# Keeping one FFN operand set on chip, and giving all attention score rows the two-bank PSUM buffers

## The chip, the cores and the metric

One core of a Trainium2 chip runs the whole kernel. The metric is the device time in microseconds (us). TensorE (PE in the rows, PEld its weight loads), VectorE (DVE), ScalarE (ACT), GpSimd (POOL) and SyncE (SP, which issues every DMA) each work through a list of instructions that was fixed when the kernel was built; they meet through semaphores.

## What is computed

One decoder layer for 1,024 positions of width 1,024, in float32. Cut to what matters here:

```
u = rmsnorm(x);  z = u @ w_in                      # input projections
y_rnn = rglru(z...);  y_att = causal_attention(...)  # 8 heads, blocks of 128 queries
h = x + concat(rmsnorm(y_rnn), rmsnorm(y_att)) @ w_out
v = rmsnorm(h)
h = h + (silu(v @ w_gate) * (v @ w_up)) @ w_down   # D_FF = 2816 = 22 blocks of 128
h = h + sigmoid(rmsnorm(h) @ w_ple_gate) * rmsnorm(p @ w_ple_proj)
out = rmsnorm(h)
```

## The kernel before, in words

**Order of the work.** Everything is recorded first as a list of operations (`Plan.add`, L203) and then ordered by `Plan.order` (L239), a list scheduler. It simulates the five engines with a cost per operation (`Plan.cost`, L167) and a latency from engine to engine (`LAT`, L133). Whenever an engine is free it takes the ready operation with the lowest place in the program whose buffers are free, and the order that comes out is what the engines get. A cost in the plan changes no instruction, only the order. `Plan.order` also hands out the buffers, of two kinds that matter here. SBUF has 51 "slots" of 128 x 1024 float32. PSUM is cut into four single banks of 512 columns (tag `bank`) and two double banks of 1024 columns (tag `wide`, `NWIDE = 2`). Every instruction is issued at L361, so the rows are told apart by the names of tiles.

**Attention** (L840 to L1050). For each of the 8 heads and each of the 8 query blocks `qb`, `scores` (L877) writes a score row of (qb+1) x 128 columns to a PSUM tile `s`: the query and the key are each split into a high and a low float32r part, so three products per 512 columns, and one 128-column bf16 product that adds the causal mask. VectorE then takes the row's maximum (`nm`), and ScalarE the exponential into `pA` (blocks 0 to 3) or `pB` (blocks 4 to 7). Rows of up to 512 columns (blocks 0 to 3) are put into a single bank, the longer ones into a double bank (L888). The single banks also hold the transposed probabilities (`tp`, copied out to `pt`), the product with the values (`av`, added into `ya`), and the query, key and value projections (`qps`, `kps`, `v`).

**The output projection.** `o_rnn` (L978) fetches the weights of output block n with `weight(("wo", n), 1)`: this block and the one behind it in the list of weights. Behind the last block of `wo` stands the first of `wpp`, which is used only after the FFN; its high and low halves stay in two slots from there on.

**The FFN** takes 22 blocks of 128 in 11 pairs p. Each 2 x 2 block product is done with seven products in place of eight (`products`, L1145): operand combinations are prepared on VectorE and ScalarE, and the seven results are added into place. For each pair, `ff_gate` and `ff_up` run seven products each; the result is two slots, from which `make_x` (L1088) prepares seven operands for the down projection, each a high and a low half in one slot named `hx` (`hilo`: an ACT copy and a DVE subtraction; four further DVE combinations, named `vt` and `silu`). `spill(p)` writes an operand to a DRAM tile, also named `hx`, one per step of the next pair's up products; for the last pair (10), whose operands have no following pair, the loop `while spill(NF // 2 - 1)` (L1283) writes all seven behind the last up product.

**The down projection** runs over chunks of pairs, `CHUNKS = ((0,1), (2,3), (4,5,6), (7,8,9,10))`. In each chunk, m = 0 to 3 runs seven products per pair of output blocks (`down`, L1238), and each product is added into the residual rows `h` on VectorE. The rows `h` come back from DRAM (`h<-hd`), two for each m of chunk 0. The operands of a chunk are fetched from DRAM (`fetch`, L1233) while the chunk before runs; those of chunk 0 during the last two up pairs (`mid_x`, L1265). The down weights `wd` are loaded and split as the products need them (`pump`). Down products also write to PSUM tiles `ff_z`, `ff_y` and `ff_x`; `ff_z` takes four of the seven products, added up in PSUM, and is read into `h` after each, so the second product into `ff_z` waits until VectorE has added the first to `h`.

All DMAs go through SP in the planned order: one that waits for its data or its slot holds up all that are behind it.

Of the kernel before, what the change touches and what calls it, by code (L numbers as in the profile page):

```python
# [19 lines left out]
HB = 512  # L20
NH = 8
DFF = 2816
NF = DFF // P
# [12 lines left out]
LAG = 3  # L36
FFW = False
CH = [slice(a, b) for a, b in [(0, 512), (512, 768), (768, 1024)]]
CHUNKS = ((0, 1), (2, 3), (4, 5, 6), (7, 8, 9, 10))
KEEP = ()  # L40
MX = (2, 4, 6)
GL = (3, 5)
NO = [0, 4, 1, 5, 2, 6, 3, 7]
# [97 lines left out]
class Plan:  # L141
# [25 lines left out]
    def cost(self, eng, fn, a, k, out):  # L167
        w = out.width() if isinstance(out, View) else 0
        if fn == "dma_start":
            v = k["out"] if isinstance(k["out"], View) else k["in_"]  # L170
            return v.shape[0] * v.width() * 4 / 360e3, 2.1
        if eng == "tensor":
            if fn == "transpose":
                return 0.108, 0.18
            return w * 0.000417 + 0.0135, 0.18
        if eng == "vector":
            if fn == "reciprocal":
                return 0.065 + w * 0.0063, 0.13
            if fn in ("tensor_reduce", "reduce_sum"):
                return 0.065 + k["in_"].width() * 0.00104, 0.13  # L180
            ptr = 0.061 * any(isinstance(x, View) for x in (k.get("scalar"), *a[2:])) if fn == "scalar_tensor_tensor" else 0.0
            one = fn in ("tensor_copy", "tensor_scalar", "tensor_scalar_mul", "tensor_scalar_add", "tensor_scalar_max")
            if one and all(v.buf.tag not in PS for v in [*a, *k.values()] if isinstance(v, View)):
                return 0.068 + w * 0.00052, 0.13
            return 0.068 + ptr + w * 0.00104, 0.13
        if eng == "scalar":
            src = k["in_"] if "in_" in k else a[1]
            c = (0.052 if src.buf.tag in PS else 0.093) + w * 0.000833
            c += 0.093 * sum(isinstance(k.get(n), View) for n in ("scale", "bias"))
            c += 0.2 * isinstance(k.get("accum_out"), View)  # L190
            return c, 0.14
        return 0.15 + w * (0.0033 if fn == "tensor_copy" else 0.0022), 0.14
# [10 lines left out]
    def add(self, eng, fn, a, k):  # L203
        o = Op()
        o.eng, o.fn, o.a, o.k, o.idx = eng, fn, a, k, len(self.ops)
        o.succ, o.npred, o.ready = [], 0, 0.0
        out = k["out"] if "out" in k else a[0]
        outs = [v for v in (out, k.get("accum_out")) if isinstance(v, View)]
        rest = list(a[1:] if "out" not in k else a) + [v for n, v in k.items() if n not in ("out", "accum_out")]
        ins = [v for v in rest if isinstance(v, View)]  # L210
        o.cost, o.lat = self.cost(eng, fn, a, k, out)
        o.port = self.shares(eng, fn, ins)
        f = k.get("func") or next((x for x in a if isinstance(x, AF)), None)
        o.table = f.name if eng == "scalar" and f is not None and f.name in FIRST else None
        preds = {self.hold: True} if self.hold else {}
        for v, w in [(v, False) for v in ins] + [(v, True) for v in outs]:
            p0, p1, c0, c1 = v.region
            keep = []
            for (q, r, qw) in v.buf.log:
                hit = r[0] < p1 and p0 < r[1] and r[2] < c1 and c0 < r[3]  # L220
                if hit and (w or qw) and q is not o:
                    preds[q] = True
                if not (w and q is not o and p0 <= r[0] and r[1] <= p1 and c0 <= r[2] and r[3] <= c1):
                    keep.append((q, r, qw))
            keep.append((o, v.region, w))
            v.buf.log = keep
        o.key = o.idx + self.shift + OFF.get(eng[0] + out.buf.name.rstrip('_ab') if isinstance(out, View) else '', 0) + (DEF if eng in ('vector', 'scalar') and not any(v.buf.tag == 'bank' for v in ins + outs) else 0)
        o.bufs = list(dict.fromkeys(v.buf for v in ins + outs))
        for b in o.bufs:
            if not b.left:  # L230
                b.first = o.idx
            b.left += 1
        for q in preds:
            q.succ.append(o)
            o.npred += 1
        self.ops.append(o)
        return o

    def order(self):  # L239
# [28 lines left out]
        while left:  # L268
            while frees and frees[0][0] <= t:
                _, _, tag, n = heapq.heappop(frees)  # L270
                free[tag] += n
            moved = False
            for e in names:
                while future[e] and future[e][0][0] <= t:
                    _, i, o = heapq.heappop(future[e])
# [5 lines left out]
                while avail[e] and tries < 40:  # L281
                    i, _, o = heapq.heappop(avail[e])
# [20 lines left out]
                o = best[2]  # L303
# [22 lines left out]
                left -= 1  # L326
                for b in o.bufs:
                    b.left -= 1
                    b.done = max(getattr(b, "done", 0.0), o.end)
                    if not b.left:  # L330
                        heapq.heappush(frees, (b.done, b.pos, b.tag, 1))
                for s in o.succ:
# [44 lines left out]
def hybrid_layer(ctx, tc, xT, pT, pos, vec, const, const2, w1, wn, wrg, wq, wkv, wo, wg, wu, *rest):  # L377
# [19 lines left out]
    def bank(name):  # L397
        return plan.tile(psp, [P, HB], F32, name, "bank", 8 - 2 * NWIDE)

    def wide(name):  # L400

        return plan.tile(psp, [P, S], F32, name, "wide", NWIDE)
# [474 lines left out]
    def scores(hd, qb):  # L877
        if qb == 0:
            pA, pA3 = slot("pA"), slot("pA3")
            st[hd] = {"p": {0: pA[:, 0:128], 1: pA[:, 128:384], 2: pA[:, 384:768], 3: pA3[:, 0:512]},  # L880
                      "rs": small([P, 8], "rs"), "nm": small([P, 8], "nm")}
        if qb >= 4:
            st[hd]["p"][qb] = slot("pB")
        pd, rs, nm = st[hd]["p"][qb], st[hd]["rs"], st[hd]["nm"]
        (qh, ql), (kh, kl) = qs[hd], ks[hd]
        n = (qb + 1) * P
        cc = slice(qb * P, (qb + 1) * P)
        ps = wide("s") if n > HB else bank("s")  # L888
        for c0 in range(0, n, HB):
            c1 = min(c0 + HB, n)  # L890
            T.matmul(ps[:, c0:c1], lhsT=qh[:, cc], rhs=kh[:, c0:c1], start=True, stop=False)
            T.matmul(ps[:, c0:c1], lhsT=qh[:, cc], rhs=kl[:, c0:c1], start=False, stop=False)
            if c1 == n:
                T.matmul(ps[:, n - P:n], lhsT=ib, rhs=mb, start=False, stop=False)
            T.matmul(ps[:, c0:c1], lhsT=ql[:, cc], rhs=kh[:, c0:c1], start=False, stop=True)
        V.tensor_reduce(out=nm[:, qb:qb + 1], in_=ps[:, :n], axis=AX.X, op=ALU.max, negate=True)
        A.activation(pd[:, :n], ps[:, :n], AF.Exp, bias=nm[:, qb:qb + 1], accum_out=rs[:, qb:qb + 1])
# [79 lines left out]

    def o_rnn(n, pss, k):  # L978
        if n not in wos:
            wos[n] = weight(("wo", n), 1)  # L980
            ops[n] = pss()
        c = slice(k * P, (k + 1) * P)
        mm(ops[n][:2], wos[n][0][:, c], wos[n][1][:, c], ys[k], k == 0, False)
# [43 lines left out]
    n = 0  # L1027
# [162 lines left out]
    def ff_up(p, mid):  # L1190
        s = sil.pop(p)
        u = [slot("ff_u"), slot("ff_u")]

        def ahead(i):
            pump("u", p)
            if i >= 3:
                if p + 1 < NF // 2:
                    pump("g", p + 1)
                else:
                    pump("d", 0)  # L1200
            if p:
                spill(p - 1)
            mid(i)

        def sink(i, ps):
            r, h = PART[i]
            v, x = u[r][:, HS[h]], s[r][:, HS[h]]
            if i < 3:
                A.activation(v, ps, AF.Copy)
            elif i == 6:  # L1210
                V.tensor_mul(x, ps, x)
            else:
                V.tensor_add(v, ps, v)
                V.tensor_mul(x, v, x)

        products(fw["u", p][0], xfs, sink, ahead)
        spilling[p] = make_x(s[0], s[1], "hx"), []
        hx[p] = spilling[p][1]


    spilling, hx = {}, {}

    def spill(p):
        steps, made = spilling[p]
# [40 lines left out]
    def mid_x(c, span):  # L1265

        ps = list(CHUNKS[c]) if c < len(CHUNKS) else []
        nxt.extend([None] * 7 for _ in ps)
        todo = [(i, k) for i in range(7) for k in range(len(ps))]
        n = len(todo)  # L1270

        def mid(m, i):
            at = span - (3 - m) * 7 - 6 + i
            while todo and (n - len(todo)) * span < at * n:
                a, k = todo.pop(0)
                nxt[k][a] = fetch(ps[k], a)
        return mid

    first = mid_x(0, 14)
    for p in range(NF // 2):  # L1280
        ff_gate(p)
        ff_up(p, (lambda i: first(p - NF // 2 + 4, i)) if p >= NF // 2 - 2 else lambda i: None)
    while spill(NF // 2 - 1):  # L1283
        pass


    hg, pacc = [], []
# [212 lines left out]
```

## Time and profile before

| | us |
|---|---|
| median of 3 runs (lowest, highest) | 1231.26 (1230.91, 1231.33) |
| the profiled execution | 1228.91 |
| its span, from the first to the last instruction | 1227.1 |
| TensorE busy in it | 1172.6 |
| VectorE, ScalarE, GpSimd busy | 990.7, 648.5, 249.8 |
| moved by DMA | 165.35 MB |

The profiled execution lies 2.35 us below the median of the runs, and its span 1.81 us below its own time; the rows are microseconds from the start of the span. The matmul rows of one instruction last longer than the distance to the next, because they are pipelined. In the windows, a granted TensorE clock of 1.00 is 2.4 GHz and 0.50 is 1.2 GHz.

### The profile page before, as it was taken

The page shows a single profiled execution, that of the slowest core. Times are in us where ns is not written, and L with a number is a line of the kernel's source. Part 1 is how long each engine was busy: PE and PEld are TensorE (multiplying, and loading weights), DVE is VectorE, ACT ScalarE, POOL GpSimd, SP SyncE. Part 2 cuts the span into 40 slices and gives each one's busy share as a digit, 9 for nine tenths or more (in the row PEclk, how much of TensorE's full clock was granted, in tenths as well). Part 3 has the DMA queues.
Part 4 walks back from the last instruction along what each step waited for, and adds up shares of the span by engine and source line. Part 5 has one row for each costly group of instructions (what it writes and reads, how often), then busy time and mean ns, then how long its engine had stood idle before and what let it go on. Part 6 is the DMA issues. An engine that isn't in the chain of part 4 may idle for free.

```text
span 1227.1 us, 15468 instructions
## 1 busy us (share of the span) xinstructions
PE 1172.6 (96%) x5608; PEld 967.8 (79%) x5608; DVE 990.7 (81%) x1486; ACT 648.5 (53%) x1086; POOL 249.8 (20%) x149
## 2 busy tenths in 40 slices
PE   8999999999999999999999999999599999999995
PEld 6788777878778878888888888888488887887894
DVE  7878777777888699988888888867689758776998
ACT  8347857777855365454454444444232213476665
POOL 0001220322101123333113332133000000243042
PEclk9999999999999999999999999999799999999998
DMA  8001100000214231453434434465998774122362
GB/s 333 18 18 35 35 1 1 1 1 1 87 69 155 103 121 54 170 189 120 172 122 160 182 124 167 155 220 188 382 374 289 276 253 176 35 103 90 117 206 87
DMA packets 50268, 165.35 MB, mean 135 GB/s; under 512 B 5648, under 2 KB 8976, under 8 KB 50192
## 3 DMA queue, kind: packets, MB, share of 16 engines
q1 hardware_dynamic: 50192, 164.37, 36.7%
q8 instruction: 44, 0.72, 0.2%
q14 instruction: 32, 0.26, 0.1%
HBM read 115.58 MB, written 48.76 MB: 134 GB/s over the span
## 4 chain that ended last, share of the span: by engine, by line
PE 76%; DVE 12%; ACT 5%; issue 3%; DMA 3%; POOL 1%; SPq 0%; DVEq 0%; ACTq 0%; POOLq 0%
PE ff_z L361 27%; PE ff_y L361 14%; PE ff_x L361 6%; PE wo L361 4%; PE plg L361 4%; PE wn L361 4%; PE s L361 3%; PE tp L361 2%; PE av L361 2%; DMA wd_r<-in_wd 2%; PE qps L361 2%; PE wn_b L361 1%; DVE h L361 1%; PE wn_a L361 1%; PE wo_a L361 1%
## 5 line engine op out<-in xcount | busy, mean ns | idle before, releaser
L361 POOL TENSOR_TENSOR silu<-silu,nf_rb 128x512 f32<-128x512 f32 x77 | 119.8, 1580 | 280.1 <-DVE silu L361 257.9
L361 PE MATMUL ff_z<-hx,wd 128*128 128x512 f32 x528 | 129.6, 393 | 9.8 <-DVE h L361 8.1
L361 PE MATMUL ff_z<-x,wg 128*128 128x512 f32 x528 | 128.0, 390 | 0.2
L361 PE MATMUL ff_z<-x,wu 128*128 128x512 f32 x528 | 127.0, 389 | 0.9 <-DVE ff_u L361 0.9
L361 PEld LDWEIGHTS ff_z<-hx,wd 128*128 128x128 f32 x528 | 99.7, 189 | 31.9 <-DVE h L361 8.8
L361 PEld LDWEIGHTS ff_z<-x,wu 128*128 128x128 f32 x528 | 99.0, 188 | 21.9 <-DVE ff_u L361 1.3
L361 PEld LDWEIGHTS ff_z<-x,wg 128*128 128x128 f32 x528 | 98.9, 188 | 21.8 <-DVE x L361 1.1
L361 DVE TENSOR_TENSOR h<-ff_z,h 128x512 f32<-128x512 f32 x64 | 44.1, 690 | 33.7 <-PE ff_z L361 25.6
L361 ACT ACTIVATE wd<-wd_r 128x256 fp32r<-128x256 f32 (+2 forms) x64 | 29.8, 490 | 73.6 <-DMA wd_r<-in_wd 26.3
L361 PE MATMUL ff_y<-hx,wd 128*128 128x512 f32 x264 | 66.3, 394 | 0.1
L361 POOL TENSOR_TENSOR p_acc<-p_acc,sq 128x1024 f32<-128x1024 f32 x7 | 18.2, 2596 | 231.8 <-ACT sq L361 231.8
L361 PE MATMUL ff_y<-x,wg 128*128 128x512 f32 x264 | 64.3, 390 | 0.9 <-ACT x L361 0.9
L361 PE MATMUL ff_y<-x,wu 128*128 128x512 f32 x264 | 63.4, 389 | 0.0
L361 PE MATMUL plg<-hg_h,wpg_l 128*128 128x256 f32 (+1 forms) x192 | 61.4, 320 | 1.3 <-DVE wpg_l L361 1.2
L361 PE MATMUL plg<-hg_h,wpg_h 128*128 128x256 f32 (+1 forms) x192 | 61.5, 320 | 0.3 <-ACT np_rb L361 0.3
L361 PE MATMUL plg<-hg_l,wpg_h 128*128 128x256 f32 (+1 forms) x192 | 61.3, 319 | 0.0
L361 PEld LDWEIGHTS ff_y<-hx,wd 128*128 128x128 f32 x264 | 50.2, 191 | 11.4 <-ACT wd L361 0.9
L361 PEld LDWEIGHTS ff_y<-x,wg 128*128 128x128 f32 x264 | 49.4, 188 | 11.7 <-ACT x L361 1.3
L361 ACT ACTIVATE wd<-wd_s 128x256 fp32r<-128x256 f32 (+2 forms) x48 | 23.3, 496 | 66.1 <-DVE wd_s L361 50.6
L361 DVE TENSOR_TENSOR pt<-tp,pt 128x512 fp32r<-128x512 f32 (+1 forms) x96 | 50.3, 549 | 9.6 <-ACT pt L361 9.3
L361 PEld LDWEIGHTS ff_y<-x,wu 128*128 128x128 f32 x264 | 49.6, 188 | 10.3
L361 DVE TENSOR_REDUCE nm<-s 128x1 f32<-128x128 f32 (+3 forms) x64 | 47.8, 752 | 11.7 <-PE s L361 10.8
(407 smaller groups left out, 3041.0 us busy)
## 6 DMA issues: line engine op xcount, KB each, us to landing
hx<-hx SPq DMA_DIRECT2D x154, 512.0 KB, 3.9
wpg_raw<-in_wpg SPq DMA_DIRECT2D x24, 512.0 KB, 3.5
wg_r<-in_wg SPq DMA_DIRECT2D x22, 512.0 KB, 4.6
wu_r<-in_wu SPq DMA_DIRECT2D x22, 512.0 KB, 4.1
wn_raw<-in_wn SPq DMA_DIRECT2D x10, 512.0 KB, 7.2
wo_raw<-in_wo SPq DMA_DIRECT2D x8, 512.0 KB, 4.0
h<-in_xT SPq DMA_DIRECT2D x8, 512.0 KB, 4.2
hd<-h SPq DMA_DIRECT2D x8, 512.0 KB, 2.9
```

Of the source, the lines that this page charges most:

```text
L361: getattr(self.engines[o.eng], o.fn)(*a, **k)
```

## The change

Four things are edited. All score rows take a double bank. In the plan's model, a matmul costs at least 0.113 us, an operation on VectorE or ScalarE whose input and output start on different partitions costs 0.11 us more, and a PSUM buffer comes free by the latency from the reading engine to TensorE. The seven operands of up pair 10 are neither written to DRAM nor fetched: they stay in their slots, and pair 10 joins pair 2 in the second down chunk (the down weights are laid out to fit, on the host). The last block of `wo` no longer asks for the first block of `wpp`, so that this is loaded with the rest of `wpp` after the FFN.

```diff
-CHUNKS = ((0, 1), (2, 3), (4, 5, 6), (7, 8, 9, 10))
-KEEP = ()
+CHUNKS = ((0, 1), (2, 10), (3, 4, 5), (6, 7, 8, 9))
+KEEP = (10,)
...
-            return w * 0.000417 + 0.0135, 0.18
+            return max(w * 0.000417 + 0.0135, 0.113), 0.18
...
+        if eng in ("vector", "scalar") and any(v.region[0] != outs[0].region[0] for v in ins if v.width() > 8):
+            o.cost += 0.11
...
-                    b.done = max(getattr(b, "done", 0.0), o.end)
+                    b.done = max(getattr(b, "done", 0.0), start + c + LAT[e, "tensor"] if b.tag in PS and e != "tensor" else o.end)
...
-        ps = wide("s") if n > HB else bank("s")
+        ps = wide("s")
...
-            wos[n] = weight(("wo", n), 1)
+            wos[n] = weight(("wo", n), 1 if n != NO[-1] else 0)
...
-            if p:
+            if p and p - 1 not in KEEP:
                 spill(p - 1)
...
-        spilling[p] = make_x(s[0], s[1], "hx"), []
+        steps = make_x(s[0], s[1], "hx")
+        if p in KEEP:
+            kept[p] = steps
+            return
+        spilling[p] = steps, []
         hx[p] = spilling[p][1]
...
-    spilling, hx = {}, {}
+    spilling, hx, kept = {}, {}, {}
...
         nxt.extend([None] * 7 for _ in ps)
-        todo = [(i, k) for i in range(7) for k in range(len(ps))]
+        nxt[:] = [kept[p] if p in KEEP else x for p, x in zip(ps, nxt)]
+        todo = [(i, k) for i in range(7) for k in range(len(ps)) if ps[k] not in KEEP]
...
-    while spill(NF // 2 - 1):
-        pass
+    for p in KEEP:
+        kept[p] = list(kept[p])
```

## Rows read from the trace of the kernel before

**Rows 1.** The page: the span, and each engine's busy time.

```profile
span 1227.1 us, 15468 instructions
PE 1172.6 (96%) x5608; PEld 967.8 (79%) x5608; DVE 990.7 (81%) x1486; ACT 648.5 (53%) x1086; POOL 249.8 (20%) x149
```

**Rows 2.** TensorE's waits, whole span: total us, times, longest.

```profile
PE ff_z L361 <- DVE h L361: 8.1, 1, 8.1
PE no_ms L361 <- DVE o_acc L361: 6.8, 1, 6.8
...
PE ff_x L361 <- DVE wd L361: 4.5, 1, 4.5
...
PE ff_z L361 <- ACT wd L361: 1.7, 1, 1.7
```

**Rows 3.** Stretches: length, engines busy (PE, PEld, DVE, ACT, POOL), clock, DMA share, GB/s.

```profile
862.80:870.60 7.80, 3.33 (x15) 2.44 (x13) 7.80 (x16) 3.67 (x6) 0.00 (x0) 1.00 0.91 358
870.60:880.28 9.68, 1.58 (x5) 0.78 (x5) 1.58 (x3) 0.00 (x0) 0.00 (x0) 0.53 0.99 369
880.28:885.30 5.02, 5.02 (x13) 4.01 (x14) 2.98 (x6) 1.47 (x4) 0.00 (x0) 0.54 1.04 423
885.30:961.00 75.70, 75.70 (x334) 62.19 (x332) 66.63 (x143) 22.88 (x57) 0.00 (x0) 1.00 0.93 344
```

**Rows 4.** Timeline, 862 to 886: start, length, instructions; in brackets the idle time before.

```profile
861.75 10.93 SPq L361 DMA_DIRECT2D hx<-hx  x9
...
862.80 1.52 PE L361 MATMUL ff_z<-hx,wd 128*128 128x512 f32 x6
...
870.61 1.58 PE L361 MATMUL ff_x<-hx,wd 128*128 128x512 f32 x4 [4.47 <-DVE wd L361]
870.79 0.70 DVE L361 TENSOR_TENSOR hx<-silu,hx 128x512 fp32r<-128x512 f32 x1
872.77 2.34 SPq L361 DMA_DIRECT2D h<-hd  x2
...
879.53 0.69 DVE L361 TENSOR_TENSOR h<-ff_z,h 128x512 f32<-128x512 f32 x1 [8.04 <-DMA h<-hd]
...
880.28 2.93 PE L361 MATMUL ff_z<-hx,wd 128*128 128x512 f32 x6 [8.09 <-DVE h L361]
```

**Rows 5.** SP's own waits, 841 to 872: total us, times, longest.

```profile
SPq L361 <- DVE hx L361: 27.7, 10, 13.6
```

**Rows 6.** The eight loads of h, 860 to 905: issue to landing.

```profile
DMA to landing us min/median/max: 6.7/7.6/8.8
```

**Rows 7.** Stretches in the attention, columns as in rows 3.

```profile
171.47:174.88 3.41, 3.41 (x11) 2.56 (x10) 0.46 (x3) 2.00 (x5) 2.37 (x1) 0.50 0.02 5
209.01:212.43 3.42, 3.42 (x13) 2.50 (x13) 2.35 (x5) 1.39 (x6) 0.00 (x0) 0.50 0.00 0
165.00:341.00 176.00, 167.59 (x982) 135.93 (x981) 138.25 (x239) 134.32 (x284) 38.52 (x24) 0.98 0.06 19
```

**Rows 8.** TensorE's waits ahead of score rows, 165 to 341.

```profile
PE s L361 <- DVE v L361: 1.8, 1, 1.8
PE s L361 <- ACT pA L361: 1.4, 3, 0.6
...
PE s L361 <- DVE ya L361: 0.8, 1, 0.8
PE s L361 <- DVE pt L361: 0.8, 2, 0.4
```

**Rows 9.** Readers of the score rows: ns min/median/max of one, first and last start.

```profile
L361 DVE TENSOR_REDUCE nm<-s x64: 280/748/1226, 167.7 to 335.5; 128x1 f32<-128x128 f32 x8, 128x1 f32<-128x256 f32 x8, 128x1 f32<-128x384 f32 x8, 128x1 f32<-128x512 f32 x8
L361 ACT ACTIVATE pA<-s,nm x32: 358/526/711, 170.5 to 320.6; 128x128 f32<-128x128 f32 x8, 128x256 f32<-128x256 f32 x8, 128x384 f32<-128x384 f32 x8, 128x512 f32<-128x512 f32 x8
...
L361 ACT ACTIVATE pB<-s,nm x32: 783/970/1133, 183.3 to 337.1; 128x640 f32<-128x640 f32 x8, 128x768 f32<-128x768 f32 x8, 128x896 f32<-128x896 f32 x8, 128x1024 f32<-128x1024 f32 x8
```

**Rows 10.** The split of the two wpp blocks on VectorE: ns min/median/max, first and last start.

```profile
L361 DVE TENSOR_TENSOR wpp_l<-wpp_raw,wpp_h x2: 1210/1218/1225, 407.5 to 1087.9; 128x1024 fp32r<-128x1024 f32 x2
```

## The prediction

> **What bounds the kernel now.** The page comes first: TensorE is busy for 1172.6 of 1227.1 us [rows 1], so all that can be won without removing matmuls is the rest, some 54 us, and what a low clock costs. I then listed what TensorE waits for [rows 2]. Of the larger waits, two (8.1 and 4.5 us) lie where the up products end and the down products begin; a third, 6.8 us for o_acc, is the tail of the kernel, which the change doesn't touch; a fourth, 1.7 us for wd, lies at the start of the fourth down chunk.
>
> The windows around the first down products [rows 3] show the place. From 862.8 to 870.6 VectorE has no free moment while TensorE works for 3.33 of 7.80 us. From 870.6 to 880.28 all compute engines all but stand still beside the DMA engines (share 0.99), and TensorE's clock is at its lower level nearly throughout. From 885.3 on TensorE has no gap for 75.7 us. The timeline says why [rows 4]. The down products start at 862.80 and stop for 4.47 us at a wd half whose subtraction stands on VectorE behind the operands of pair 10. The next product into ff_z must wait until the first has been added to h. The h rows are only asked for at 872.77: on SP their loads stand behind nine hx transfers, from 861.75 on. The load lands 6.7 us after its issue (the shortest of eight) [rows 6], the addition starts at 879.53, and TensorE goes on at 880.28 after 8.09 us [rows 4]. SP itself is held up by VectorE: between 841 and 872 it spends 27.7 us in ten waits for hx operands that it is to write out [rows 5]. The last operand of pair 10 is made at 870.79 to 871.49, and only then can its write go out, with the h loads behind it. So this stall is a queue on SP whose head waits for VectorE.
>
> **Part 1: pair 10 stays on chip.** Seven writes and seven reads of 512 KB leave SP's queue, each with its wait; no instruction on TensorE, VectorE or ScalarE goes. The h loads then stand behind the fourteen fetches of chunk 0 alone. Those need slots that the up products give back as they end, so the last can go out near 863, and the h loads right behind. With the same 6.7 us they land near 870 [rows 6]. What is late next is VectorE: its subtractions for pair 10 keep their place in the program and end at 871.5 [rows 4]. The addition to h takes 0.69 us, so TensorE takes up ff_z at about 872.3 instead of 880.28: 8.0 us. The 4.47 us wait for wd stays, since the work ahead of it on VectorE is unchanged.
>
> The clock: before, it is at 0.53 and 0.54 in the windows where TensorE works for 1.58 and 5.02 us [rows 3], which costs 0.47 x 1.58 + 0.46 x 5.02 = 3.0 us. After a wait of 4.47 us I expect one short drop still. The shortest in these rows is 3.41 us at 0.50 [rows 7], worth 1.7 us, so 1.3 us come back. Sum for this part: 9.3 us.
>
> Bounds: nothing, if the planner issues the h loads no earlier, since it fixes SP's order from its own model; up to 4.5 + 8.1 + 3.0 = 15.6 us if the new order also brings the wd subtraction ahead of pair 10's. I take 9.3, because VectorE's queue of 7.8 us without a gap [rows 3] is untouched. A loss is bounded by slots: seven stay taken from about 871 to the end of the second chunk. But that chunk needs these operands in slots anyway, seven fetches for it fall away, and the two wpp slots come free.
>
> The 1.7 us at the fourth chunk [rows 2] depends on 28 fetches, all still there: 0 to 1.7, taken as 0.
>
> **Part 2: wpp later.** One load, one ScalarE copy and one VectorE subtraction of 1.22 us [rows 10] move from about 400 us to just before the products that use them. On SP the load passes all FFN loads and stands between p and the second wpp block. The second block's subtraction is the row at 1087.9, and TensorE is at down products until about 1090, which covers it. Without that cover the cost is the 1.22 us of VectorE. I take 0; range 0 to 1.2 us lost.
>
> **Part 3: score rows in double banks, and the new costs in the plan.** No instruction changes. TensorE idles 8.4 us of the 176 in the attention [rows 7]. Of that, 4.8 us are score rows of up to 512 columns that wait until a single bank has been read by another engine: v, ya, pt and pA name its earlier holder [rows 8]. The clock is low twice, for 3.41 and 3.42 us [rows 7], which costs 1.7 us each time; in both stretches TensorE worked without a gap. The most that can be won is 8.4 + 3.4 = 11.8 us.
>
> Against it stands the new wait. A short row now needs one of two double banks, and on TensorE's list everything behind it waits with it: the transposes, the value products, the next projections. From the readers' rows, a buffer is held for reduction and exponential: about 0.28 + 0.36 to 0.69 + 0.71 us for short rows and up to 1.23 + 1.13 for long ones [rows 9], and the matmuls ahead of these. I estimate 2 us for a short and 3.7 us for a long row: 32 x 3.7 = 118 us of 2 x 176 us before, 182 us of it after, so 34% becomes 52%. The double banks aren't full, and VectorE and ScalarE, at 138 and 134 of 176 us [rows 7], set the pace of a row. I take 3.5 us won: two single waits gone (1.8 and 0.8 us), one low-clock stretch less (1.7), and 0.8 us of new waits. Ends: 11.8 us won, and the loss of rival 3.
>
> A rule speaks against this part. The Trainium skill ("TensorE: Matmul & The Clock Gate", section "A second HAM failure mode: psum-queue depth-cycling") says that a kernel which cycles through PSUM buffers, with short idle times between groups of matmuls, can see its clock go down and up again and again. Two buffers in turn for 64 rows are such a cycle. The trace has only two drops in eight heads, in spite of seven short waits [rows 8], so it bears that out weakly. By that rule the 1.7 us counted above would go and the 10 us of drops in rival 3 would come.
>
> **Sum.** 9.3 + 0 + 3.5 = 12.8 us. The profiled execution took 1228.91 us, 1.8 more than its span and 2.35 less than the median, so it would become 1216.1, and the median 1231.26 becomes 1218.5.
>
> **Rivals.**
> (1) The attention gains more: with four banks free for transposes and value products, most of its idle time and both drops go, 10 us instead of 3.5. For it: nearly all the larger waits for score rows are for single banks. Against: VectorE and ScalarE are near 80%. Time: 1212.
> (2) The stall only moves: the h loads go out earlier but land behind full DMA queues (share 0.91 to 1.04 [rows 3]), or VectorE adds to h only after further wd halves. Then 3 of the 9.3 us are won; with 3.5 from the attention, 1225.
> (3) Slower: the double banks become the wait. Each of 32 short rows holds TensorE until one comes free. The gain of part 1 is used up at 9.3 / 32 = 0.29 us per row. At 0.4 us per row it is 12.8 us, and with a clock drop in each of the eight heads instead of two in all, another 6 x 1.7 = 10 us: 1231.26 - 9.3 + 23 = 1245. For it: the occupation rises by half. Against: at 52% one of the two is mostly free, and the planner knows when.
> (4) The change doesn't do what it says: pair 10 stays on chip, but SP's planned order keeps the h loads behind slots that are late. About 1231.
>
> **How the numbers follow.** My forecast has 0.55, rival 1 0.17, rival 2 0.13, rival 3 0.09, rival 4 0.06. The first alone spans 1213 to 1224. For 8 in 10 the range takes in rivals 1 and 2, the first with 11.8 us in the attention and 10.8 in part 1 as its far end, the second with nothing in the attention: 1208 to 1229. 0.2% is 2.5 us, about what a measurement of this kernel can tell from no change. Faster by over that: forecast, rival 1, and nearly all of rival 2, 0.84. Within: rival 4 and some of rival 2, 0.07. Slower: rival 3, 0.09.
>
> **What would show it.** In the changed profile, SP's waits for hx between the last up and the first down products should be fewer by seven, with the h loads issued near 863 to 866. The wait of ff_z for h should be under 2 us, with the wait of ff_x for wd still near 4.5, and the low-clock stretch after it short. HBM traffic should fall by 14 x 512 KB. In the attention, waits of s should name exponentials of score rows alone, and their sum should stay under 4 us. It would be wrong if the wait for h stays above 5 us, or if TensorE's idle time between 165 and 341 grows.

## The result, and the profile after

The changed kernel takes 1209.14 us (median of 4 runs, 1206.05 to 1209.53) against 1231.09 us for the kernel before in the same session: a ratio of 0.9819, 95% interval 0.9801 to 0.9838. It is 22.0 us faster. The forecast was 1218.5 us, 12.8 us faster, with a range of 1208 to 1229.

The page of the profiled execution (1206.05 us, the fastest of the four), the lines that answer to [rows 1], and its HBM line:

```profile
span 1204.2 us, 15416 instructions
PE 1164.7 (97%) x5608; PEld 965.5 (80%) x5608; DVE 985.5 (82%) x1486; ACT 645.5 (54%) x1086; POOL 250.8 (21%) x149
HBM read 111.91 MB, written 45.09 MB: 130 GB/s over the span
```

TensorE does the same 5608 matmuls and is busy for 7.9 us less; that is a first hint of where the forecast was short. HBM reads are down from 115.58 to 111.91 MB and writes from 48.76 to 45.09 MB, 3.67 MB each, seven operands of 512 KB.

TensorE's waits over the whole span (total us, times, longest), against [rows 2]:

```profile
PE no_ms L364 <- DVE o_acc L364: 6.7, 1, 6.7
...
PE ff_z L364 <- DVE h L364: 5.2, 2, 4.2
...
PE ff_z L364 <- ACT wd L364: 0.9, 1, 0.9
```

The wait for h has halved, and the wait of ff_x for wd is gone. The timeline at the first down products, against [rows 4]:

```profile
846.80 1.62 SPq L364 DMA_DIRECT2D h<-hd  x2
...
849.30 1.52 PE L364 MATMUL ff_z<-hx,wd 128*128 128x512 f32 x6
...
850.60 0.42 DVE L364 TENSOR_TENSOR wd<-wd_r,wd 128x256 fp32r<-128x256 f32 x1
...
852.02 1.52 PE L364 MATMUL ff_x<-hx,wd 128*128 128x512 f32 x6
...
856.35 0.69 DVE L364 TENSOR_TENSOR silu<-silu,vt 128x512 f32<-128x512 f32 x1
...
856.95 0.69 DVE L364 TENSOR_TENSOR h<-ff_z,h 128x512 f32<-128x512 f32 x1
...
857.70 2.93 PE L364 MATMUL ff_z<-hx,wd 128*128 128x512 f32 x6 [4.15 <-DVE h L364]
```

The h loads go out 2.5 us before the first down product, where before it was 10 us after it. The first wd half that ff_x was late for is now split ahead of pair 10's operands, so ff_x runs at once. The addition to h starts when VectorE has done the operand ahead of it, with no idle time between.

SP's own waits for operands that it is to write out, from 828 to 858, a stretch that lies around the first down product as that of [rows 5] does:

```profile
SPq L364 <- DVE hx L364: 2.3, 3, 1.3
```

Ten such waits (27.7 us) have become three.

The stretches, columns as in [rows 3]: the attention, from the first score product to the end of the last row's maximum, the low-clock stretch at the down products, and all from 10.67 us to the next fall of the clock, with that fall in the last row.

```profile
168.40:323.40 155.00, 153.32 (x942) 127.94 (x941) 131.33 (x232) 125.63 (x273) 36.07 (x22) 1.00 0.05 16
...
857.18:860.59 3.41, 2.89 (x7) 2.32 (x8) 2.33 (x5) 1.92 (x5) 0.00 (x0) 0.50 1.02 414
...
10.67:352.00 341.33, 333.14 (x1779) 275.32 (x1778) 286.50 (x440) 243.41 (x416) 55.05 (x30) 1.00 0.12 46
352.00:355.41 3.41, 2.89 (x7) 2.31 (x8) 3.41 (x4) 2.75 (x3) 0.00 (x0) 0.50 0.00 0
```

For the same stretch of the attention, the kernel before shows:

```profile
167.10:336.80 169.70, 161.29 (x946) 130.58 (x945) 132.49 (x232) 129.14 (x275) 36.81 (x22) 0.98 0.05 16
```

So this stretch is 14.7 us shorter, and the clock no longer falls in it. But it doesn't hold quite the same work: six products of the value projection (`v`) that lie inside it before, behind the first score product, stand ahead of its start after, which is 1.4 us. Stretches with the same work, 1100 matmuls in either kernel (the rows count two more at the edges), go from the first `v` product to the first product that uses the attention's result (`wo<-ya_h`), first before, then after:

```profile
165.13:366.57 201.44, 190.54 (x1102) 154.59 (x1100) 157.97 (x270) 145.95 (x302) 38.39 (x24) 0.98 0.07 24
164.97:352.52 187.55, 183.32 (x1102) 152.46 (x1100) 156.33 (x270) 144.41 (x302) 37.75 (x24) 1.00 0.08 26
```

This is the gain of the attention without work that only moved: 13.9 us, of which 6.7 are idle time (10.9 against 4.2) and 7.2 busy time of the same matmuls. From the first down product to the first product of the per-layer embedding (`ple`), the kernel before took 228.1 us (862.80 to 1090.89) and the changed one 218.4 (849.30 to 1067.68).

### The profile page after: what moved, and what is told of

Read it like the earlier page. It is cut to its first block, busy times and chain, and to the rows that moved or that the text cites. A ratio compares the mean times of both kernels' runs of the same rounds, so it can differ in the third digit from the quotient of the medians.

```text
span 1204.2 us, 15416 instructions
## 1 busy us (share of the span) xinstructions
PE 1164.7 (97%) x5608; PEld 965.5 (80%) x5608; DVE 985.5 (82%) x1486; ACT 645.5 (54%) x1086; POOL 250.8 (21%) x149
## 3 DMA queue, kind: packets, MB, share of 16 engines
HBM read 111.91 MB, written 45.09 MB: 130 GB/s over the span
## 4 chain that ended last, share of the span: by engine, by line
PE 82%; DVE 10%; ACT 3%; issue 2%; DMA 2%; SPq 0%; DVEq 0%; ACTq 0%
PE ff_z L364 28%; PE ff_y L364 14%; PE ff_x L364 7%; PE plg L364 6%; PE wo L364 5%; PE s L364 4%; PE wn L364 4%; PE av L364 2%; PE tp L364 2%; PE qps L364 2%; DMA wd_r<-in_wd 2%; PE wn_b L364 1%; DVE h L364 1%; PE wn_a L364 1%; PE wo_a L364 1%
## 5 line engine op out<-in xcount | busy, mean ns | idle before, releaser
L364 ACT ACTIVATE wu<-wu_r 128x512 fp32r<-128x512 f32 x44 | 27.6, 627 | 59.2 <-DVE wu_r L364 28.1
```

Of the source, the lines that this page charges most:

```text
L364: getattr(self.engines[o.eng], o.fn)(*a, **k)
```

## The experiments

"Before" below is always the kernel before, run on the same chip in the same session; its median was 1229.99 to 1230.29 us in the three sessions. The attention is timed from the first score product to the end of the last row's maximum, the down stage from the first down product to the first ple product.

### The double banks alone

```diff
-        ps = wide("s") if n > HB else bank("s")
+        ps = wide("s")
```

> The kernel before, with all score rows in the double banks and nothing else. Theory A (the single banks were the attention's limit): the output projection's first product with the attention's result starts 10 to 14 us earlier than before (366.6 us), waits of s for readers of v, ya and pt are gone, the total falls by 10 to 14 us. Theory B (the plan's new costs made the gain, the buffers alone are worth little): that start moves by under 4 us, the total by under 4 us or up, since the planner still thinks narrow matmuls shorter than they are. The wait at the first down products stays near 12.6 us in both.

1220.74 us, ratio 0.9915 (0.9882 to 0.9948), about 10 us faster. The attention fell from 169.6 to 156.3 us. Its window, that of the 1100 matmuls, and TensorE's waits in the first:

```profile
170.70:327.10 156.40, 154.22 (x946) 128.42 (x945) 131.29 (x233) 125.88 (x275) 36.01 (x22) 1.00 0.05 15
167.31:356.16 188.85, 183.80 (x1101) 152.52 (x1100) 156.62 (x270) 144.33 (x302) 36.02 (x23) 1.00 0.08 26
```

```profile
PE tp L361 <- DVE k_l L361: 0.8, 2, 0.5
PE v L361 <- DVE v L361: 0.5, 1, 0.5
PE tp L361 <- DVE ya L361: 0.4, 1, 0.4
```

No score row waits any more [rows 8], and no new wait for a double bank has come. The same 1100 matmuls take 188.85 us where they took 201.44: 12.6 us less, 5.9 of it idle time and 6.7 busy time. The first product with the attention's result starts at 356.2 instead of 366.6, 10.4 us earlier: in this profile the attention itself starts 2.2 us later, behind a low-clock stretch (3.41 us from 152.51) that the profile before doesn't have. Theory A stands, with the total at its lower end: this one line makes nearly all of the attention's gain. The waits of 12 us at the down products were still there (4.5 and 7.3 us).

### The plan's new costs alone

```diff
-            return w * 0.000417 + 0.0135, 0.18
+            return max(w * 0.000417 + 0.0135, 0.113), 0.18
...
+        if eng in ("vector", "scalar") and any(v.region[0] != outs[0].region[0] for v in ins if v.width() > 8):
+            o.cost += 0.11
...
-                    b.done = max(getattr(b, "done", 0.0), o.end)
+                    b.done = max(getattr(b, "done", 0.0), start + c + LAT[e, "tensor"] if b.tag in PS and e != "tensor" else o.end)
```

> The kernel before, with the three edits of the plan's model and nothing else. Theory A: the attention ends within 4 us of before, the waits of s for v, ya and pt are still there. Theory B: it ends 10 to 14 us earlier, with those waits mostly gone. The wait at the first down products stays near 12.6 us in both.

1230.12 us, ratio 0.9998 (0.9981 to 1.0014): nothing. The attention took 170.4 us (the 1100 matmuls 201.44, exactly as before), with the waits for single banks grown where the reader is a score row's exponential:

```profile
PE s L364 <- ACT pA L364: 4.0, 5, 1.0
PE s L364 <- ACT q_h L364: 1.6, 1, 1.6
PE s L364 <- DVE v L364: 1.5, 1, 1.5
PE qps L364 <- ACT pA L364: 1.4, 1, 1.4
```

A better model of the durations did not find an order that the buffers don't allow. Theory B falls.

### The kept pair alone

```diff
-CHUNKS = ((0, 1), (2, 3), (4, 5, 6), (7, 8, 9, 10))
-KEEP = ()
+CHUNKS = ((0, 1), (2, 10), (3, 4, 5), (6, 7, 8, 9))
+KEEP = (10,)
...
-    while spill(NF // 2 - 1):
-        pass
+    for p in KEEP:
+        kept[p] = list(kept[p])
```

> The kernel before, with pair 10 kept on chip in the second chunk and nothing else (wpp still loaded early, old costs, short score rows in single banks). Theory A (the h loads stood behind writes on SP that waited for VectorE): the total falls by 8 to 11 us, all of it between the first and the last product of chunk 0, and the attention is as before. Rival (the removal works only with the two slots of wpp or the new order): under 4 us, since the h loads still go out after 868 us.

1222.97 us, ratio 0.9943 (0.9926 to 0.9959): 7.0 us faster. The down stage fell from 228.1 to 222.6 us in the profiled execution, which was the slowest of its runs (1225.84). TensorE's waits from 840 to 1000, and its low-clock stretch:

```profile
PE ff_x L361 <- DVE wd L361: 4.5, 1, 4.5
PE ff_y L361 <- DVE h L361: 0.9, 1, 0.9
```

```profile
870.51:877.34 6.83, 4.49 (x11) 3.52 (x12) 5.00 (x11) 1.70 (x4) 0.00 (x0) 0.50 1.03 413
```

The wait of 8.1 us for h is gone and the one of 4.5 us for wd stays, as the prediction had it; the first h load goes out at 864.86, 0.2 us before the first down product, and lands 6.7 us later. The gain lies under the 8 to 11 us of theory A, though well above the rival's 4. In this profile two things are short of what was forecast. TensorE's idle time in the down stage fell by 6.0 us (from 14.4 to 8.4), not by 8.0. And the clock stays low for 6.83 us, not for one 3.41, and falls again for 3.41 us at 1010.46: TensorE works for 4.49 and 3.41 us of these, which costs 4.0 us against 3.0 before, where 1.3 were to come back.

### Double banks and costs together

```diff
-CHUNKS = ((0, 1), (2, 10), (3, 4, 5), (6, 7, 8, 9))
-KEEP = (10,)
+CHUNKS = ((0, 1), (2, 3), (4, 5, 6), (7, 8, 9, 10))
+KEEP = ()
...
-            wos[n] = weight(("wo", n), 1 if n != NO[-1] else 0)
+            wos[n] = weight(("wo", n), 1)
```

(against the changed kernel)

> The changed kernel without the kept pair and without the later load of wpp: double banks and new costs alone. If the parts add, the total is 11 to 14 us under the kernel before and the waits of the first down products are near 12.6 us again. If score rows and costs work against each other apart and gain only together, this run is faster than both single ones together.

1217.75 us, ratio 0.9897 (0.9873 to 0.9921), 12.4 us faster. The attention took 154.9 us, 1.4 less than with the double banks alone, so the costs are worth that much once the buffers are there (the 1100 matmuls: 187.48 against 188.85). The totals of the two runs differ by 3.0 us; the other 1.6 can't be told from the spread of the double banks' own executions (1215.32 to 1222.68). The waits at the down products were 4.5 and 7.9 us. With the 7.0 us of the kept pair the parts add up to 19.4 of the 22.0 us; the rest is no larger than the intervals of the three ratios, 2 to 3 us to either side.

### The first wpp block, early or late

Two runs: the changed kernel with the early load, and the kernel before with the kept pair and the late load.

```diff
-            wos[n] = weight(("wo", n), 1 if n != NO[-1] else 0)
+            wos[n] = weight(("wo", n), 1)
```

> The changed kernel with the first wpp block loaded early again, so that its two halves hold two slots through the FFN. If the later load is worth nothing by itself (my prediction), the total stays within 2 us of the changed kernel and TensorE has no wait of over 2 us for wd. Rival: the two free slots let SP's fetches and wd loads go earlier, and it was this that removed the 4.5 us wait for wd and shortened the low clock; then that wait is back and the stretch from the first down product to the first ple product grows from 218.4 to near 222.6 us, as in the run with the kept pair alone.

> The kernel before with the kept pair and the later load of wpp, short score rows in single banks and old costs. If the two slots make the difference of 4 us between the kept pair alone (222.6 us from the first down product to the first ple product) and the changed kernel (218.4), it is near 218.4 here, and the wait for wd is gone. If the new costs make it, it stays near 222.6 with the 4.5 us wait for wd.

They took 1209.33 us (0.9824, 0.9789 to 0.9859) and 1222.31 us (0.9928, 0.9905 to 0.9951), within 1 us of the changed kernel and of the kept pair alone. TensorE's waits from 800 to 1090, first with the early, then with the late load:

```profile
PE ff_x L364 <- DVE wd L364: 4.5, 1, 4.5
PE ff_z L364 <- ACT wd L364: 2.6, 1, 2.6
```

```profile
PE ff_z L361 <- DVE h L361: 4.3, 2, 3.9
PE ff_z L361 <- ACT wd L361: 0.9, 1, 0.9
```

So this edit decides which of two waits stands at the first down products: with the early load it is wd, with the late one h, and the two cost about the same in the total. The profiled down stages said more than that, 222.65 us with the early load against 218.38 and, for the other pair, 222.63 against 217.63. But the executions profiled with the late load were the fastest of their runs, and the times don't bear out 4 us. I first read the profiles as the rival's gain; the run that follows corrected it.

### The changed kernel again

> The changed kernel unaltered, for a second profile and more times, since its first profiled execution (1206.05 us) was 3 us faster than its other three. If the 4.3 us that the run with wpp loaded early lost from the first down product to the first ple product (222.65 against 218.38 us) were a property of the kernels, this one is again near 218.4; if it is the spread between executions of a stage that is full of transfers, it is anywhere up to 222.

1208.70 us, ratio 0.9834 (0.9814 to 0.9854); the profiled execution took 1208.98. Its down stage is 220.4 us, with the same wait for h (4.13 us) but a low clock there for 6.83 us instead of 3.41, and 1.2 us more idle time in all (7.3 against 6.1). So this stage differs by 2 us between executions of one kernel, and differences of that size between single profiles of it say nothing.

### The writes put back, in place and later

Seven writes of pair 10's operands, which nobody reads, recorded right behind the operands, or behind the first seven down products:

```diff
+    def write(p):
+        for a, x in enumerate(kept[p]):
+            dr = plan.tile(drm, [P, S], F32, f"hx{p}_{a}", f"hx{p}_{a}", 1)
+            Y.dma_start(out=dr, in_=f(x[0].whole))
...
     for p in KEEP:
         kept[p] = list(kept[p])
+        write(p)
```

and, for the later place, in the loop over m instead:

```diff
+            if c == 0 and m == 0:
+                for p in KEEP:
+                    write(p)
```

> The changed kernel, which in addition writes pair 10's seven operands to DRAM where they were written before, ahead of the h loads on SP; nobody reads them. Theory A (order on SP): the h loads go out after the last operand is made again, the wait of ff_z for h goes from 4.2 back to 8 or more, and the total rises by 5 to 10 us. Rival (DMA traffic): seven of the fourteen transfers are back, so about half of the gain, 4 to 5 us, is lost here and in the run with the writes behind the h loads alike.

> As the run with the writes in place, but recorded behind the first seven down products, so that the h loads of these are ahead of them on SP. Theory A: the wait for h stays near 4.2 us and the total within 2 us of the changed kernel, with the same traffic as the other run. Rival (traffic): 4 to 5 us are lost, as in the other run.

In place: 1217.37 us (0.9885, 0.985 to 0.9919), 8.7 us over the changed kernel's second run, which was in another session. Later: 1210.14 us (0.9833, 0.9792 to 0.9874), 1.4 us over it. Both write 48.76 MB. The timelines, in place first:

```profile
857.56 0.69 DVE L364 TENSOR_TENSOR hx<-silu,hx 128x512 fp32r<-128x512 f32 x1 [0.76 <-ACT hx L364]
...
858.69 1.90 SPq L364 DMA_DIRECT2D h<-hd  x2
...
864.91 0.69 DVE L364 TENSOR_TENSOR h<-ff_z,h 128x512 f32<-128x512 f32 x1 [6.66 <-DMA h<-hd]
...
865.66 2.93 PE L364 MATMUL ff_z<-hx,wd 128*128 128x512 f32 x6 [12.33 <-DVE h L364]
```

```profile
847.43 2.16 SPq L364 DMA_DIRECT2D h<-hd  x2
...
858.07 2.93 PE L364 MATMUL ff_z<-hx,wd 128*128 128x512 f32 x6 [4.13 <-DVE h L364]
```

In place, the h loads wait again for the last operand (857.56 to 858.25) and go out at 858.69, 11 us later than with the writes behind them. The wait for h is 12.33 us against 4.13. In one session, the same writes cost 7.2 us more ahead of the h loads than behind them, so it was the order on SP. The rival of the traffic falls, but for what may be in the 1.4 us, which the intervals don't tell from nothing.

### What is left at the first down products

Pair 10's operands put later in the planner's order, and then in addition the first two h loads asked for earlier:

```diff
     for p in KEEP:
+        plan.shift = 400
         kept[p] = list(kept[p])
+        plan.shift = 0
```

> The changed kernel, with the preparation of pair 10's operands put 400 places later in the planner's order, so that VectorE takes the first additions to h and the wd halves ahead of it. The h load landed at 855.55 and the addition started at 856.95 us, so if VectorE's order is what is left (my prediction's reading), the wait of ff_z for h falls from 4.2 us by up to 1.4 us, and no more, the landing being next; total 0 to 2 us under the changed kernel. Rival (the landing alone sets it): no difference.

1207.62 us (0.9823, 0.9804 to 0.9842), 1.1 us under the changed kernel in the same session; the wait for h is 3.3 us, down from 4.1. As expected, VectorE's order was the last thing, by 0.8 us of that wait. The low clock behind it was shorter too (3.41 us against 6.83), so the total doesn't tell the two apart.

```diff
+    def mid_up(p, i):
+        if p == NF // 2 - 1 and i == 4:
+            for n in (0, 1):
+                hs[n] = slot("h")
+                Y.dma_start(out=hs[n], in_=hd[n])
+        first(p - NF // 2 + 4, i)
...
-            if c == 0 and i == 0:
+            if c == 0 and i == 0 and m:
```

> As the run before, with the two h loads of the first down products also asked for two products earlier, in the last up pair. If landing and VectorE's order are the two things that are left, the wait of ff_z for h, 4.2 us, goes to under 1 us, the low-clock stretch with it, and the total falls by 3 to 6 us under the changed kernel. Rival (the fetches of chunk 0 that now come later are needed as early): the wait comes back at a product that waits for its operand, and the total is within 2 us.

1205.05 us (0.9803, 0.9782 to 0.9824), 3.7 us under the changed kernel in the same session (its five runs, 1203.17 to 1206.44, all lie below that kernel's four): faster than both kernels. The h loads go out 5.6 us before the first down product. TensorE's waits from 800 to 1090, and the window of the first down products:

```profile
PE ff_z L364 <- ACT wd L364: 3.8, 3, 2.0
PE ff_z L364 <- ACT hx L364: 1.1, 1, 1.1
PE ff_z L364 <- DVE h L364: 0.8, 2, 0.6
```

```profile
849.00:875.00 26.00, 23.90 (x101) 18.14 (x100) 24.54 (x52) 9.75 (x23) 0.00 (x0) 1.00 0.98 387
```

The clock doesn't fall here any more. The next wait is for an operand (1.1 us), and then wd at the later chunks.

### Three single banks

The double banks alone, with one single bank fewer:

```diff
-        return plan.tile(psp, [P, HB], F32, name, "bank", 8 - 2 * NWIDE)
+        return plan.tile(psp, [P, HB], F32, name, "bank", 7 - 2 * NWIDE)
```

> The kernel before with all score rows in double banks and one single bank fewer, three for everything else; only the attention is compared (169.6 us before, from the first score row's product to the last row's maximum; 156.3 with four single banks). If the score rows' own use of single banks was the limit because there are too few of them, three without score rows are little better than four with them: 163 to 170 us. If it was the in-order wait of score rows for a bank that a reader still held, three banks do as well as four: under 159 us.

The attention took 169.7 us, as long as before with four single banks and the short rows in them, and the 1100 matmuls 206.6 against 201.4 (one profile; the stages around it lose time too, so its total of 1247.73 us isn't compared). The waits in the attention are now those of the other users, the first a query projection:

```profile
PE qps L361 <- DVE k_l L361: 1.8, 1, 1.8
...
PE qps L361 <- DVE ya L361: 1.3, 3, 0.5
```

Taking one bank from the transposes, value products and projections costs at least as much as letting the short rows in. So these users need a fourth single bank, and it fits that the gain came from the rows leaving theirs. What share the rows' own in-order waits had in it isn't told apart by this run.

## Why the prediction was right or wrong

**The direction and the range held, the range by 1.1 us at its lower end; the size was off by 9 us, and the term that failed is part 3.** I had 3.5 us for the attention, with 11.8 as "the most that can be won"; over the same 1100 matmuls it was 13.9 in either profile of the changed kernel, 12.6 of it by the buffers alone. The step that failed first is the choice of what would go: "two single waits gone (1.8 and 0.8 us), one low-clock stretch less (1.7), and 0.8 us of new waits". Idle time fell by 6.7 us and not 2.6. Both low-clock stretches went, 3.4 us by the prediction's price. And the new wait, a short row held up until a double bank is free, came to none. Behind this choice stood that VectorE and ScalarE "set the pace of a row". They had room: in the attention's window they were busy for 132 and 129 of 169.7 us before, and are for 131 and 126 of 155.0 after.

The second step that failed is the bound, by 2.1 us. I took all of TensorE's busy time in [rows 7] as work and only the 8.4 us beside it as waiting. The same 1100 matmuls were busy for 7.2 us less after the change; 3.4 us of that is the low clock, and the other 3.8 the prediction had at nothing. Most likely it is waiting that doesn't show as idle, since the row of a matmul lasts beyond the start of the next and so covers a short gap behind it (after, from 347.34 on, the rows of the `wo` products last 0.39 us and start 0.22 to 0.23 us apart). No run shows this by itself.

**Rival 3 and the rule.** By the rule of the Trainium skill ("TensorE: Matmul & The Clock Gate", section "A second HAM failure mode: psum-queue depth-cycling") the clock could have gone down more often with two buffers in turn. The trace disagrees here: over the 1100 matmuls the granted clock is 1.00 in both profiles of the changed kernel and with the double banks alone, where it fell twice before [rows 7]. That the waits for the single banks had made it fall is likely, but isn't settled: the run with the kept pair and the late load of wpp had the short rows in single banks too, and in its attention the clock fell only once. And the gain in the clock isn't whole. In both profiles of the changed kernel it falls for 3.41 us right behind, from 352.00 and from 351.83, within a wait of 2.55 us ahead of the first product with the attention's result; before, with nearly the same wait (2.49 us) there, it did not.

**Rival 1** had the right cause, as far as the run with three single banks tells (more single banks for transposes and value products), and 10 us, still below what was measured.

**Part 1** was right in mechanism: SP's order, with writes ahead that wait for VectorE, as the two runs with the writes put back show. In size I had 9.3 us. Alone it measured 7.0, with the h loads issued and landing as forecast and the low clock mis-sized; on top of the other parts 1217.75 became 1208.70 to 1209.14, 8.6 to 9.0 us across sessions. That this is so near 9.3 is luck: three steps in it were off there, and nearly cancelled. The h loads went out 2.5 us before the first down product and not at its start or later, but the first took 8.7 us to land and not 6.7. "The 4.5 us wait for wd stays" holds with wpp early and not with wpp late, where the plan puts the wd half first and the wait for h is 4.1 us in its place; the prediction had said under 2. And the low clock lasted 3.41 us in one profile but 6.83 in others. That VectorE's queue would be what is late next was right, by 0.8 us (operands put later).

**Part 2** at no cost: its total can't be told from nothing (1209.33 against 1208.70 and 1209.14), as predicted, but the edit isn't without effect: it exchanges one wait for the other.

**The new costs** were counted within part 3 and are worth nothing by themselves, and 1.4 us with the double banks.

## What to carry to other kernels

Don't take an engine's busy row as its work when the rows overlap: compare the busy time of the same instructions in two stretches, or bound a gain by both idle time and the spread of busy time. Take care that they are the same: a stretch between two events can lose work at its edges, here six products and 1.4 us. Where a fixed list of DMAs is issued by one queue, look at what its head waits for: moving seven writes behind two loads was worth 7 us at equal traffic. And before refining a scheduler's costs, ask whether the buffers allow a better order at all; here the refined costs won nothing until one kind of tile got its own.

## What was not expected of the hardware

Asked for earlier, the first h load landed no earlier, as counted from the first down product. With the kept pair alone it is issued 0.2 us before that product and takes 6.7 us; in the changed kernel it is issued 2.5 us before it and takes 8.7. So it lands 6.5 us behind the product in the one and 6.3 in the other. The DMA engines are full in the changed kernel (share 1.02 at 410 GB/s from 849.30 to 857.20), but they were before as well (0.99 and 1.04 [rows 3]); what makes the earlier load take longer isn't shown. In the run with both edits of the last step it is issued 5.6 us before the product, takes 7.0 us and lands 1.4 us behind it. And the clock's low stretch after a wait of about 4.1 us lasted 3.41 us in one execution of the changed kernel and 6.83 in another.
